# Deferred query/key evictions, column-scalar normalisation steps and later weight casts in a two-layer encoder trunk

## The chip, the cores and the metric

The kernel runs on one core of one Trainium2 chip. The metric is the device time of one execution in microseconds (us). The kernel before was timed three times; the profile is one further execution of the same program. For a kernel of this kind and this spread of runs, about 0.5% (8.4 us) is what a comparison can tell from no change.

## The reference

Two layers over x of 512 rows and 1024 columns, conditioned on one vector c, all in float32:

```
for l in range(2):
    mod = silu(c) @ w_ada[l] + b_ada[l]             # shift1, scale1, gate1, shift2, scale2, gate2
    h = layer_norm(x) * (1 + scale1) + shift1
    proj = h @ w_in[l]                              # q/k/v of 3 head groups | pooling | 2 gates
    outs, lses = dilated_band_attention(...)        # 3 groups, rates 1, 4, 16, centred band, ALiBi
    att = sum(softmax(lses) * outs)                 # groups combined by their denominators
    y_att, y_pool = att @ w_att_out[l], pooled @ w_pool_out[l]
    merged = sigmoid(gate_att) * y_att + sigmoid(gate_pool) * y_pool
    x = layer_norm(ALPHA * x + (1 + gate1) * (merged @ w_o[l]), ln1_g, ln1_b)
    h2 = layer_norm(x) * (1 + scale2) + shift2
    a, b = split(h2 @ w_ffn_in[l])
    x = layer_norm(ALPHA * x + (1 + gate2) * ((silu(a) * b) @ w_ffn_out[l]), ln2_g, ln2_b)
```

## The kernel before

Every weight product is done in three matmuls: each operand is split into a high part (rounded to the matrix engine's float32r form by a cast on ScalarE) and a low part (the rest, by a subtraction on VectorE, `split`, lines 197 to 199), and the matmuls are high by high, high by low and low by high (`mm3`). A weight chunk is 128 by 1024 numbers, loaded by SyncE's queue into one of six `raw` buffers; `weights()` keeps loads seven chunks ahead and splits three chunks ahead. For `w_o` and `w_ffn_out` GpSimd first multiplies the raw chunk by the gate row (line 100).

A *slot* is one projection of 128 output channels over 512 rows: 24 matmuls of 512 columns into one of four PSUM banks called `mm`. `slot()` (line 121) is called ahead of each; it issues what was deferred to it (`self.later`), then one step of every running attention generator (`self.attn`), then a piece of the adaLN product (`self.ada`, line 205). The order in which these Python calls issue instructions is the order in which each engine runs them: nothing reorders it, and an engine that waits holds up all that is behind it.

Stages of a layer, in order: values; pooling; `qk` and attention (four pairs of heads j, six projections q0, k0, q1, k1, q2, k2 each, with the attention of pair j spread over the following eight slots); gates; `merge`; `tail` of the mixing sub-layer; `ffn_in`; `tail` of the feed-forward. An attention step does, among other things, transposes of the probabilities of one block of the step before on TensorE (lines 591 and 601), score matmuls (559 to 565), a masking reduction on VectorE (577) and the exponentials on ScalarE (581). In `qk` a projection's result is evicted from PSUM by ScalarE and VectorE as soon as it has been issued: `query_tiles` (499, 482, 484), `key_tiles` (474, 475, 482, 484, and copies on GpSimd, 491 and 493), `pair_queries` (506, 507), `pair_keys` (GpSimd memsets 517, then 519, 521).

`merge` (line 757) makes eight slots m; after the last gate projection it splits `w_o` chunks 0 to 5 ahead (`prefetch(7, 6)`, line 770), then VectorE multiplies and adds (773, 774), and the merged tile is split. `tail` runs the product with all weights resident, for four row tiles t, by a written script (`TAIL_MIX`, `TAIL_FFN`, `TAIL_END`): `g` is the six matmuls of one weight chunk for one t (794), `c` one step of that t's normalisation `chain` (826), `h` takes the next weight chunk, `n` half a projection of the next stage, which uses the part of h that is ready. The chain's column work is `rstd` (251): a square root on ScalarE (256), then on VectorE four tiny instructions on one number per partition (257, 258, 260, 264), a Newton step of the reciprocal root; then `nm * r` (856), the full-row normalisation on ScalarE (857), transposes (280), scale and shift (867), and the high and low parts of h (868, 872). While the bridge runs, splits of feed-forward chunks have their subtraction on GpSimd (199), not on VectorE.

Of the kernel before, what the change touches and what calls it, by code (L numbers as in the profile page):

```python
# [15 lines left out]
ALU = mybir.AluOpType  # L16
# [13 lines left out]
KD = D // P  # L30
# [18 lines left out]
class Net:  # L49
# [71 lines left out]
    def slot(self):  # L121
        due, keep = [], []
        for e in self.later:
            e[0] -= 1
            (due if e[0] <= 0 else keep).append(e)
        self.later = keep
        for e in due:
            e[1]()
        self.attn = [g for g in self.attn[::-1] if next(g, True) is None][::-1]
        while self.ada:  # L130
            if next(self.ada[0], True) is None:
                break
            self.ada.pop(0)
# [117 lines left out]
    def rstd(self, ss, n=1, scale=1.0 / D):  # L251
        nc = self.nc
        r = self.t("rs", [P, n], F32, 4)
        ve = self.t("ve", [P, n], F32, 4)
        tmp = self.t("nt", [P, n], F32, 4)
        nc.scalar.activation(r, ss, AF.Sqrt, bias=self.eps, scale=scale)
        nc.vector.tensor_scalar(ve, ss, -0.5 * scale, -0.5 * EPS, op0=ALU.mult, op1=ALU.add)
        nc.vector.reciprocal(r, r)
        if n == 1:
            nc.vector.scalar_tensor_tensor(tmp, r, ve, r, op0=ALU.mult, op1=ALU.mult)  # L260
        else:
            nc.vector.tensor_mul(tmp, r, ve)
            nc.vector.tensor_mul(tmp, tmp, r)
        nc.vector.scalar_tensor_tensor(r, tmp, 1.5, r, op0=ALU.add, op1=ALU.mult)  # L264
        return r

    def new_h(self):
# [255 lines left out]

    def qk(self, l, j):
        out = {}
        for nm in ("q0", "k0", "q1", "k1", "q2", "k2"):
            self.slot()
            pb = self.bank()
            self.proj(pb, self.weights(), self.h, range(KD))
            if nm == "k0":  # L530
                out[nm] = self.key_tiles(pb)
            elif nm == "q0":
                out[nm] = self.query_tiles(pb, j)
            elif nm[0] == "q":
                out[nm] = self.pair_queries(pb, self.qsc[:, 4 + j : 5 + j])
            else:
                out[nm] = self.pair_keys(pb)
        return out

    def attention(self, j, x, res):  # L540
# [216 lines left out]
    def merge(self, l, att, ty):  # L757
        nc = self.nc
        out = []
        for m in range(8):  # L760
            self.slot()
            if m % 2 == 0:
                wa = self.weights()
                sg = self.g([P, 2, S])
            pg = self.bank()
            self.proj(pg, self.weights(), self.h, range(KD))
            s = sg[:, m % 2]
            nc.scalar.activation(s, pg, AF.Sigmoid)
            if m == 7:
                self.prefetch(7, 6)  # L770
            py = self.bank()
            self.proj(py, wa, lambda k: att[k], range(4), woff=(m % 2) * S)
            nc.vector.tensor_mul(s, s, py)
            nc.vector.tensor_add(s, s, ty[m])
            mg = self.g([P, 2, S], F32R)
            self.split(mg[:, 0], mg[:, 1], s)
            out.append(mg)
        self.drain()
        return out
# [46 lines left out]
    def chain(self, t, acc, x, g, b, dst, nxt):  # L826
        nc = self.nc
        z, hn = self.g([P, D]), self.g([P, D])
        sm = self.t("sm", [P, 2], F32, 4)
        half = [slice(hf * S, hf * S + S) for hf in range(2)]  # L830
        for hf, c in enumerate(half):
            nc.vector.scalar_tensor_tensor(z[:, c], x[:, c], ALPHA, acc[hf], op0=ALU.mult, op1=ALU.add, accum_out=sm[:, hf : hf + 1])
        nm = self.t("nm", [P, 1], F32, 4)
        ss = self.t("ss", [P, 1], F32, 4)
        nc.vector.tensor_scalar(nm, sm[:, 0:1], sm[:, 1:2], -1.0 / D, op0=ALU.add, op1=ALU.mult)
        nc.scalar.activation(hn, z, AF.Square, bias=nm, scale=1.0, accum_out=ss)
        yield
        nc.vector.scalar_tensor_tensor(x, z, nm, g, op0=ALU.add, op1=ALU.mult)
        yield
        r = self.rstd(ss)  # L840
        yield
        if nxt is None:
            for c in half:
                nc.vector.scalar_tensor_tensor(z[:, c], x[:, c], r, b[:, c], op0=ALU.mult, op1=ALU.add)
                nc.sync.dma_start(out=dst[:, c], in_=z[:, c])
            return
        sm2 = self.t("sm", [P, 2], F32, 4)
        nc.vector.scalar_tensor_tensor(z, x, r, b, op0=ALU.mult, op1=ALU.add, accum_out=sm2[:, 0:1])
        nc.gpsimd.dma_start(out=dst, in_=z)
        nm = self.t("nm", [P, 1], F32, 4)  # L850
        ss = self.t("ss", [P, 1], F32, 4)
        nc.vector.tensor_scalar(nm, sm2[:, 0:1], -1.0 / D, None, op0=ALU.mult)
        nc.scalar.activation(hn, z, AF.Square, bias=nm, scale=1.0, accum_out=ss)
        yield
        r = self.rstd(ss)
        nc.vector.tensor_mul(nm, nm, r)
        nc.scalar.activation(hn, z, AF.Identity, bias=nm, scale=r)
        yield
        pbs = self.h_turn(hn)
        yield  # L860
        tmp = [self.t("q0", [P, 4, P], F32, 2) for _ in range(2)]
        l, which = nxt
        for q in range(2):
            for i in range(4):
                m = 16 * which + 8 * q + 2 * i
                sh, sc = self.mod[:, l, m : m + 1], self.mod[:, l, m + 1 : m + 2]
                nc.vector.tensor_scalar(tmp[q][:, i, :], pbs[q][:, i * P : i * P + P], sc, sh, op0=ALU.mult, op1=ALU.add)
            nc.scalar.copy(self.hA[q][:, :, 0, t * P : t * P + P], tmp[q])
            yield
        for q in range(2):  # L870
            hh = self.hA[q][:, :, :, t * P : t * P + P]
            nc.vector.tensor_sub(hh[:, :, 1], tmp[q], hh[:, :, 0].bitcast(F32))
            yield
# [128 lines left out]
def layout(i):  # L1002
# [20 lines left out]
        "w_ada": c(ada),  # L1023
        "b_col": c(b_col),
        "w_in": c(np.concatenate([v12, v0, qk, rest], axis=1)),
        "w_mix": c(i["w_pool_mix"].transpose(0, 2, 1, 3)),
        "p_col": c(i["pool_scale"].reshape(L, 4, P).transpose(2, 0, 1)),
# [24 lines left out]
```

## Time and profile before

| | us |
|---|---|
| three timed runs | 1685.62, 1688.78, 1692.08 (median 1688.78) |
| the profiled execution | 1687.45 |
| its span (first to last instruction) | 1685.7 |

| engine | busy us | share of the span |
|---|---|---|
| TensorE matmuls (PE) | 1646.1 | 98% |
| TensorE weight loads (PEld) | 1375.5 | 82% |
| VectorE (DVE) | 959.2 | 57% |
| ScalarE (ACT) | 667.3 | 40% |
| GpSimd (POOL) | 336.3 | 20% |

Matmuls overlap: one of 512 columns is shown as 0.39 us, and the next starts about 0.23 us after it. So the busy share of PE counts no time twice, but the time that can go is in the stretches in which the next matmul starts late. The row of PE's waits gives these by what ended them.

### The profile page before, as it was taken

To read this page: it belongs to the slowest core of one execution; us is meant where nothing else is said; L and a number is where in the kernel's file an instruction comes from. 1 tells how busy PE (TensorE), PEld (TensorE's weight loads), DVE (VectorE), ACT (ScalarE), POOL (GpSimd) and SP (SyncE) were. 2 spreads that over 40 slices of the span, in tenths; PEclk is the share of its full clock that TensorE was granted. 3 is DMA by queue.
4 is the path that set the end of the run, shared out by engine and by line. 5 is a ranking of instruction groups with operands and counts; after the bars stand their busy time and mean duration, and the time that the engine had idled before them with its cause. 6 is when DMAs were issued, how large, how long until landed. Compare 5 with 4: busy or idle time off the path is not lost.

```text
span 1685.7 us, 21107 instructions
## 1 busy us (share of the span) xinstructions
PE 1646.1 (98%) x8162; PEld 1375.5 (82%) x8162; DVE 959.2 (57%) x1628; ACT 667.3 (40%) x1118; POOL 336.3 (20%) x325
## 2 busy tenths in 40 slices
PE   8999999999989999999999999999999999999998
PEld 6888887888788888888878888888887888888886
DVE  7568777437775554333573787763477753333335
ACT  6356455623443222221442655555234422222212
POOL 2003222003240000345230122210042300004440
PEclk9999999999999999999999999999999999999999
DMA  9525445233534555332522254443334344233341
GB/s 335 174 75 185 154 138 176 89 100 101 187 100 135 191 189 172 101 112 95 205 90 79 88 188 143 146 156 108 100 113 150 126 154 139 95 100 100 106 144 50
DMA packets 63799, 227.20 MB, mean 135 GB/s; under 512 B 7681, under 2 KB 8097, under 8 KB 63698
## 3 DMA queue, kind: packets, MB, share of 16 engines
q1 hardware_dynamic: 55296, 199.25, 35.4%
q0 software_dynamic: 8400, 26.59, 4.8%
q8 instruction: 64, 1.05, 0.3%
q14 instruction: 37, 0.30, 0.1%
q10 hardware_dynamic: 2, 0.00, 0.0%
HBM read 217.28 MB, written 8.54 MB: 134 GB/s over the span
## 4 chain that ended last, share of the span: by engine, by line
PE 82%; DVE 10%; ACT 5%; issue 2%; DMA 0%; POOL 0%; SPq 0%; DVEq 0%; ACTq 0%
PE mm L239 18%; PE mm L241 18%; PE mm L240 18%; PE mm L794 9%; PE pt L794 5%; PE s L794 4%; PE mm L396 2%; PE mm L625 2%; DVE w L199 2%; PE pt L396 2%; ACT w L198 1%; DVE g L199 1%; DVE nt L260 1%; DVE rs L264 1%; DVE raw L205 1%
## 5 line engine op out<-in xcount | busy, mean ns | idle before, releaser
L239 PE MATMUL mm<-h,w 128*128 128x512 f32 (+1 forms) x1440 | 557.4, 387 | 0.0
L241 PE MATMUL mm<-h,w 128*128 128x512 f32 (+1 forms) x1440 | 554.2, 385 | 1.1 <-DVE w L199 1.1
L240 PE MATMUL mm<-h,w 128*128 128x512 f32 (+1 forms) x1440 | 554.1, 385 | 0.0
L199 DVE TENSOR_TENSOR w<-raw,w 128x1024 fp32r<-128x1024 f32 x238 | 313.8, 1332 | 183.6 <-ACT w L198 183.6
L198 ACT CAST w<-raw 128x1024 fp32r<-128x1024 f32 x250 | 255.5, 1043 | 172.3 <-PE mm L794 145.9
L241 PEld LDWEIGHTS mm<-h,w 128*128 128x128 f32 x1440 | 270.6, 188 | 56.2 <-DVE w L199 1.9
L239 PEld LDWEIGHTS mm<-h,w 128*128 128x128 f32 x1440 | 270.8, 188 | 53.4 <-issue 1.0
L240 PEld LDWEIGHTS mm<-h,w 128*128 128x128 f32 x1440 | 270.8, 188 | 51.8
L100 POOL TENSOR_TENSOR raw<-raw,g 128x1024 f32<-128x1024 f32 x60 | 153.9, 2574 | 376.4 <-DMA raw<-w_ffn_out 222.4
L198 ACT CAST g<-g 128x512 fp32r<-128x512 f32 x76 | 47.1, 620 | 307.2 <-DVE g L890 228.1
L890 DVE TENSOR_TENSOR g<-g,mm 128x512 f32<-128x512 f32 x42 | 28.9, 688 | 211.6 <-PE mm L241 207.4
L794 PE MATMUL mm<-w,g 128*128 128x512 f32 x600 | 143.3, 389 | 0.0
L794 PEld LDWEIGHTS mm<-w,g 128*128 128x128 f32 x600 | 112.6, 188 | 23.3
L205 DVE SCALAR_TENSOR_TENSOR raw<-raw,silc 128x1024 f32<-128x1024 f32 x96 | 118.2, 1237 | 1.4 <-DMA raw<-w_ada 1.4
L199 DVE TENSOR_TENSOR g<-g,g 128x512 fp32r<-128x512 f32 x76 | 66.0, 868 | 62.0 <-ACT g L198 62.0
L794 PE MATMUL s<-w,g 128*128 128x512 f32 x300 | 75.6, 391 | 3.9 <-ACT w L198 2.8
L794 PE MATMUL pt<-w,g 128*128 128x512 f32 x300 | 74.3, 389 | 0.0
L794 PEld LDWEIGHTS s<-w,g 128*128 128x128 f32 x300 | 56.0, 188 | 17.0 <-ACT w L198 3.6
L491 POOL CAST kp<-kp 64x640 fp32r<-64x640 f32 x16 | 21.1, 1342 | 241.0 <-ACT kp L482 241.0
L794 PEld LDWEIGHTS pt<-w,g 128*128 128x128 f32 x300 | 56.3, 188 | 11.7
L232 POOL DMA_DIRECT2D dg<-gr x4 | 2.2, 546 | 295.5 <-DVE gr L230 295.5
L889 ACT ACTIVATE g<-mm 128x512 f32<-128x512 f32 x42 | 25.2, 599 | 85.1 <-PE mm L241 85.1
(233 smaller groups left out, 2061.0 us busy)
## 6 DMA issues: line engine op xcount, KB each, us to landing
raw<-w_in SPq DMA_DIRECT2D x112, 512.0 KB, 3.3
raw<-w_ada SPq DMA_DIRECT2D x96, 512.0 KB, 4.5
raw<-w_ffn_in SPq DMA_DIRECT2D x88, 512.0 KB, 3.4
raw<-w_ffn_out SPq DMA_DIRECT2D x44, 512.0 KB, 3.2
raw<-w_o SPq DMA_DIRECT2D x16, 512.0 KB, 3.3
xs<-g POOLq DMA_DIRECT2D x12, 512.0 KB, 3.0
g<-xs POOLq DMA_DIRECT2D x12, 512.0 KB, 6.4
g<-d POOLq DMA_DIRECT2D x16, 256.0 KB, 4.9
```

Source lines behind the costliest of these rows:

```text
L100: self.nc.gpsimd.tensor_mul(self.raws[i], self.raws[i], self.gate[info(i)][0])
L198: self.nc.scalar.copy(dst_hi, src)
L199: (self.nc.gpsimd if pool else self.nc.vector).tensor_sub(dst_lo, src, dst_hi.bitcast(F32))
L205: self.nc.vector.scalar_tensor_tensor(raw, raw, 1.0, self.silc, op0=ALU.mult, op1=ALU.mult, accum_out=self.mod[:, l, m : m + 1])
L239: mm(out, lhsT=whi, rhs=xhi, start=first, stop=False)
L240: mm(out, lhsT=whi, rhs=xlo, start=False, stop=False)
L241: mm(out, lhsT=wlo, rhs=xhi, start=False, stop=last)
L396: nc.tensor.matmul(pv[p, g], lhsT=hh[:, hi, tk], rhs=w[k][wi][:, c], start=k == 0 and i == 0, stop=k == KD - 1 and i == 2)
L625: nc.tensor.matmul(o, lhsT=v, rhs=rhs, start=b == 0, stop=b == 1)
L794: mm(acc[t][hf], lhsT=src[k][:, part, tk], rhs=wx[:, hf * S : hf * S + S], start=k == 0 and part == 0 and wi == 0, stop=k == K - 1 and par ...
L889: nc.scalar.activation(tmp[:, 0], pa, AF.Silu)
L890: nc.vector.tensor_mul(tmp[:, 1], tmp[:, 0], pb)
```

## The change

Four edits in one:

1. `slot()` steps the attention generators ahead of the deferred work instead of behind it.
2. `qk` defers each eviction by one slot. With edit 1 an eviction stands behind the attention step of the following slot, where it stood ahead of that step. The matmul order does not change.
3. `rstd` for one column, and `nm * r`, use `tensor_scalar` with per-partition scalar operands instead of `scalar_tensor_tensor` and `tensor_mul`. The count of instructions is the same.
4. At the end of `merge`, three `w_o` chunks (2, 3, 4) instead of four are split ahead of the last multiply and add; chunks 5 and 6 are split behind these and ahead of the last merged tile, where chunk 6 came behind the tile.

```diff
@@ slot
         self.later = keep
+        self.attn = [g for g in self.attn[::-1] if next(g, True) is None][::-1]
         for e in due:
             e[1]()
-        self.attn = [g for g in self.attn[::-1] if next(g, True) is None][::-1]
@@ rstd
         if n == 1:
-            nc.vector.scalar_tensor_tensor(tmp, r, ve, r, op0=ALU.mult, op1=ALU.mult)
+            nc.vector.tensor_scalar(tmp, r, ve, r, op0=ALU.mult, op1=ALU.mult)
+            nc.vector.tensor_scalar(r, tmp, 1.5, r, op0=ALU.add, op1=ALU.mult)
         else:
             nc.vector.tensor_mul(tmp, r, ve)
             nc.vector.tensor_mul(tmp, tmp, r)
-        nc.vector.scalar_tensor_tensor(r, tmp, 1.5, r, op0=ALU.add, op1=ALU.mult)
+            nc.vector.scalar_tensor_tensor(r, tmp, 1.5, r, op0=ALU.add, op1=ALU.mult)
@@ qk
-        for nm in ("q0", "k0", "q1", "k1", "q2", "k2"):
-            self.slot()
-            pb = self.bank()
-            self.proj(pb, self.weights(), self.h, range(KD))
+
+        def evict(nm, pb):
             if nm == "k0":
                 out[nm] = self.key_tiles(pb)
...
+        for nm in ("q0", "k0", "q1", "k1", "q2", "k2"):
+            self.slot()
+            pb = self.bank()
+            self.proj(pb, self.weights(), self.h, range(KD))
+            self.defer(1, lambda nm=nm, pb=pb: evict(nm, pb))
         return out
@@ merge
             if m == 7:
-                self.prefetch(7, 6)
+                self.prefetch(7, 5)
             py = self.bank()
             self.proj(py, wa, lambda k: att[k], range(4), woff=(m % 2) * S)
             nc.vector.tensor_mul(s, s, py)
             nc.vector.tensor_add(s, s, ty[m])
+            if m == 7:
+                self.prefetch(7, 7)
             mg = self.g([P, 2, S], F32R)
@@ chain
         r = self.rstd(ss)
-        nc.vector.tensor_mul(nm, nm, r)
+        nc.vector.tensor_scalar(nm, nm, r, None, op0=ALU.mult)
```

The first place is ScalarE in layer 0, in the third slot of pair j=2's projections (q1), where attention j=1 does its third step: `kp_1866` and `kp_1871` are k0's tiles, `pt_1884` the transposed probabilities and `g_1896` the exponentials of block 2. Before:

```order
L198 CAST w_1838<-raw_1563 128x1024
L474 COPY kp_1866<-mm_1835 128x4x64
L482 CAST kp_1871<-kp_1866 64x640
L482 CAST kp_1872<-kp_1866 64x640
L595 COPY g_1883<-pt_1884 128x512
L581 ACTIVATE g_1896,st_1731<-g_1896,st_1731 128x256 x4
L198 CAST w_1928<-raw_1628 128x1024
```

And now, with k0's tiles as `kp_1905` and `kp_1910`, the exponentials as `g_1879`, and q0's eviction (`q_324_1825`, `g_1827`) shown ahead because it stands one step later too:

```order
L500 ACTIVATE q_324_1825<-mm_1756,qsc 128x512
L483 CAST g_1827<-q_324_1825 64x512 x2
L198 CAST w_1838<-raw_1563 128x1024
L600 COPY g_1866<-pt_1867 128x512
L586 ACTIVATE g_1879,st_1721<-g_1879,st_1721 128x256 x4
L475 COPY kp_1905<-mm_1835 128x4x64
L483 CAST kp_1910<-kp_1905 64x640
L483 CAST kp_1911<-kp_1905 64x640
L198 CAST w_1928<-raw_1628 128x1024
```

Three instructions of k0's eviction went from ahead of the exponentials to behind them. VectorE's share of the eviction (copy 475, subtractions 484) moved in the same way behind the masking reductions, and the weight split stays last in the slot.

The second place is VectorE at the end of `merge` in layer 0: `raw_3507`, `raw_3557`, `raw_3566`, `raw_3617`, `raw_3649` and `raw_3700` (now `raw_3705`) are `w_o` chunks 2 to 7, `g_3564` is the sum that becomes the last merged tile, `g_3683` (now `g_3688`) that tile. Before:

```order
L199 TENSOR_TENSOR g_3653<-raw_3507,g_3652 128x1024
L199 TENSOR_TENSOR w_3657<-raw_3557,w_3656 128x1024
L199 TENSOR_TENSOR w_3661<-raw_3566,w_3660 128x1024
L199 TENSOR_TENSOR w_3665<-raw_3617,w_3664 128x1024
L773 TENSOR_TENSOR g_3564<-g_3564,mm_3668 128x512
L774 TENSOR_TENSOR g_3564<-g_3564,g_3135 128x512
L199 TENSOR_TENSOR g_3683<-g_3564,g_3683 128x512
L199 TENSOR_TENSOR w_3709<-raw_3649,w_3708 128x1024
L199 TENSOR_TENSOR g_3715<-raw_3700,g_3714 128x1024
```

And now:

```order
L199 TENSOR_TENSOR g_3652<-raw_3507,g_3651 128x1024
L199 TENSOR_TENSOR w_3656<-raw_3557,w_3655 128x1024
L199 TENSOR_TENSOR w_3660<-raw_3566,w_3659 128x1024
L778 TENSOR_TENSOR g_3564<-g_3564,mm_3663 128x512
L779 TENSOR_TENSOR g_3564<-g_3564,g_3135 128x512
L199 TENSOR_TENSOR w_3681<-raw_3617,w_3680 128x1024
L199 TENSOR_TENSOR w_3685<-raw_3649,w_3684 128x1024
L199 TENSOR_TENSOR g_3688<-g_3564,g_3688 128x512
L199 TENSOR_TENSOR g_3715<-raw_3705,g_3714 128x1024
```

The split of chunk 5 went behind the multiply and add, and that of chunk 6 ahead of the merged tile's. ScalarE's casts stand in the same order, so there too chunk 6's cast is no longer behind the cast that waits for the add.

## Rows read from the trace of the kernel before

**Rows 1.** PE's waits over the span: total us, times, longest us.
```profile
PE s L280 <- ACT g L857: 6.6, 4, 2.8
PE pt L240 <- DVE h L872: 5.5, 2, 2.7
PE pt L601 <- ACT g L581: 5.0, 8, 0.7
...
PE s L794 <- ACT w L198: 2.8, 2, 1.6
...
PE s L794 <- DVE w L199: 1.1, 2, 0.5
```

**Rows 2.** PE's waits in 820 to 870 us, the feed-forward tail of layer 0.
```profile
PE s L280 <- ACT g L857: 2.6, 2, 1.6
PE pt L396 <- DVE h L872: 1.3, 1, 1.3
PE pt L396 <- ACT h L868: 0.7, 1, 0.7
```

**Rows 3.** Busy times by stretch, with the granted clock (PEclk).
```profile
424.00:440.00 16.00, 13.90 (x54) 10.69 (x53) 12.61 (x11) 6.62 (x8) 4.96 (x4) 0.90 0.86 310
440.00:500.00 60.00, 54.48 (x313) 48.30 (x312) 47.96 (x112) 27.59 (x42) 19.46 (x12) 0.97 0.34 113
```

**Rows 4.** Timeline of PE, transposes of block 2: start us, us, instruction, idle before.
```profile
166.56 0.60 PE L601 MATMUL pt<-ident,g 128*128 128x128 f32 x4
...
211.77 0.33 PE L601 MATMUL pt<-ident,g 128*128 128x128 f32 x1 [0.57 <-ACT g L581]
212.76 0.82 PE L601 MATMUL pt<-ident,g 128*128 128x128 f32 x3 [0.66 <-ACT g L581]
```

**Rows 5.** Timeline of ACT just ahead of the second of these.
```profile
207.06 1.48 ACT L482 CAST kp<-kp 64x640 fp32r<-64x640 f32 x2 [2.21 <-DVE kp L475]
...
211.12 0.51 ACT L581 ACTIVATE g<-g,st 128x256 f32<-128x256 f32 x1 [1.98 <-DVE st L577]
```

**Rows 6.** Timeline of PE where merge ends and the tail begins, layer 0.
```profile
428.85 4.24 PE L794 MATMUL s<-w,g 128*128 128x512 f32 x18
434.66 0.73 PE L794 MATMUL s<-w,g 128*128 128x512 f32 x2 [1.57 <-ACT w L198]
435.92 1.32 PE L794 MATMUL s<-w,g 128*128 128x512 f32 x4 [0.53 <-DVE w L199]
```

**Rows 7.** Timeline of DVE at the same place.
```profile
426.71 3.48 DVE L199 TENSOR_TENSOR w<-raw,w 128x1024 fp32r<-128x1024 f32 x3
...
430.83 2.18 DVE L774 TENSOR_TENSOR g<-g,g 128x512 f32<-128x512 f32 x1
```

**Rows 8.** Timeline of POOL at the same place.
```profile
429.13 3.33 POOL L100 TENSOR_TENSOR raw<-raw,g 128x1024 f32<-128x1024 f32 x1 [4.57 <-DVE w L199]
```

**Rows 9.** Timeline of DVE in the mixing tail of layer 0.
```profile
470.62 0.15 DVE L852 TENSOR_SCALAR nm<-sm 128x1 f32<-128x1 f32 x1
470.69 2.71 DVE L872 TENSOR_TENSOR h<-q,h 128x512 fp32r<-128x512 f32 x1
...
474.16 1.51 DVE L260 SCALAR_TENSOR_TENSOR nt<-rs,ve 128x1 f32<-128x1 f32 x1
475.71 2.27 DVE L264 SCALAR_TENSOR_TENSOR rs<-nt,rs 128x1 f32<-128x1 f32 x1
...
478.10 0.68 DVE L872 TENSOR_TENSOR h<-q,h 128x512 fp32r<-128x512 f32 x1
...
482.10 1.75 DVE L260 SCALAR_TENSOR_TENSOR nt<-rs,ve 128x1 f32<-128x1 f32 x1
483.88 2.34 DVE L264 SCALAR_TENSOR_TENSOR rs<-nt,rs 128x1 f32<-128x1 f32 x1
```

**Rows 10.** Timeline of POOL over the first of these.
```profile
469.83 8.15 POOL L199 TENSOR_TENSOR w<-raw,w 128x1024 fp32r<-128x1024 f32 x3 [12.53 <-ACT w L198]
```

**Rows 11.** Groups of DVE by form: count, busy us, mean ns.
```profile
L835 DVE TENSOR_SCALAR nm<-sm 128x1 f32<-128x1 f32 x16 | 3.4, 215 | 0.6
```

## The prediction, made blind

> **What bounds the kernel now.** I read PE's waits first. TensorE sets the end nearly throughout, so time goes only where its next matmul starts late. Of those waits the change can touch five kinds [rows 1]: transposes of attention probabilities that wait for exponentials (L601, eight waits, 5.0 us), the tail's transposes that wait for a normalised row (L280, four, 6.6 us), the bridge's matmuls that wait for a low part of h (L240, two, 5.5 us), and the first tail products that wait for a `w_o` chunk's cast or subtraction (L794, 2.8 and 1.1 us, once each a layer). The feed-forward tail of layer 0 holds 2.6 us of the L280 waits and 2.0 us of its own [rows 2]; so the two mixing tails hold 6.6 - 2.6 = 4.0 of L280 and all 5.5 of L240. Then I read the granted clock: it is 0.90 over the 16 us in which merge ends and 0.97 over the 60 us of the tail behind it, where 1.00 is full speed [rows 3]. At half speed a matmul takes double, so 0.10 x 16 = 1.6 us and 0.03 x 60 = 1.8 us went there; both stretches hold long waits of TensorE, and the fall goes with them.
>
> **Attention (edits 1 and 2).** Four undisturbed transposes of block 2 take 0.60 us. At 211.77 they start 0.57 late and last 212.76 + 0.82 - 211.77 = 1.81, so the pair of waits costs 0.57 + 1.21 = 1.78 us [rows 4]. The eight waits are four such pairs: 7.1 us. ACT shows why: behind k0's two casts, for which it idled 2.21 us and worked 1.48, the exponentials started at 211.12, after a further 1.98 us in which it waited for the reduction on VectorE, itself behind k0's subtractions [rows 5]. TensorE had asked at 211.77 - 0.57 = 211.2. With the eviction behind the step, the 2.21 us of waiting and the 1.48 of casts leave the path of the exponentials. Against that, q0's eviction, which stood ahead of the step before, now falls into the end of that slot: two casts and two subtractions, which I put at the length of k0's casts, 1.48 us. Net 2.21 + 1.48 - 1.48 = 2.2 us earlier, more than the 1.78 that a pair costs. What is late next: the eviction itself and the weight split behind it. The evicted bank is written again only after another projection of 24 matmuls (4.24 / 18 x 24 = 5.7 us [rows 6]) and the next step's scores, and the split is for two slots ahead, so both are covered by about a slot; without that cover each would cost what it comes late. The order in GpSimd's queue changes too: the statistics exchange now stands ahead of k0's copies, whose reader is a later attention. SP's queue is the same. Bounds: 7.1 us gained to 2 us lost (a late split, four times, at the 0.5 us that the one for chunk 6 cost [rows 6]). I take 6.3, nearest to the pair's own price, less 0.2 a pair because the next step's exponentials come closer to TensorE's request.
>
> **End of merge (edit 4).** TensorE waits 1.57 us for chunk 6's cast, 0.53 for its subtraction [rows 6]. Both stand behind the add L774, which took 2.18 us because it ran while GpSimd scaled chunk 7, 429.13 to 432.46 [rows 7, 8]. In the new order chunk 6's cast no longer waits for the add. VectorE has one split fewer ahead of it (3.48 / 3 = 1.16 us each [rows 7]), so it reaches the add earlier, but the add still ends with GpSimd's scaling, which itself waits for a raw buffer; I expect it about 1 us earlier, at 431.5 instead of 433.0. Then come the splits of chunks 5 and 6, 432.7 and 433.8. At 0.23 us a matmul and six a chunk TensorE wants chunk 5's low part at 432.0 and chunk 7's at 435.4, where I get 435.6. So 0.9 us of waiting stays of 2.1 in layer 0, and about 0.5 of 1.7 in layer 1 (2.8 + 1.1 less layer 0's 2.1 [rows 1]). Gain 1.2 + 1.2, and 1.6 of clock in layer 0, since no gap over 1 us is left: 4.0. The two row loads ahead of the tail now stand behind chunk 6's scaling in GpSimd's queue; their first reader is L838, over 10 us later. Bounds: 2.8 + 1.1 + 1.6 = 5.5 gained, to 1 lost if chunk 5, now behind the add, comes as late as chunk 6 did.
>
> **Column forms (edit 3).** Two of the tiny instructions take 1.51 and 2.27 us at 474.16 [rows 9], under three GpSimd subtractions that run from 469.83 to 477.98 [rows 10]: VectorE's operations on two tensors in SBUF get in only between those, at 475.67 and 477.98. L852, a `tensor_scalar` in the same GpSimd stretch, takes 0.15 while the L872 right behind it takes 2.71 [rows 9]. The new forms should take what L835 takes, a `tensor_scalar` with a per-partition operand: 0.215 us [rows 11]. The pair then ends at 474.6, not 477.98, and the L872 that TensorE waits for starts at the next gap, 475.7, instead of 478.10: 2.4 of the 2.7 us of that wait. Twice, 4.8. In the last chain of the tail the pair takes 1.75 + 2.34 [rows 9]; 3.66 us of it goes, but the full-row operation behind is itself on two tensors, so it gains about 2.4, and a third blocked instruction of 1.5 us ahead of L857 goes too. That is about 4 us of chain against an L280 wait of 2.8 in layer 0, where TensorE itself comes 2.4 earlier: I take 2.4 us there and 1.2 in layer 1, its whole wait. With 1.2 of the clock's 1.8 us in layer 0 (the stretch's waits get short), 4.8 + 3.6 + 1.2 = 9.6. Bounds: 5.5 + 4.0 + 1.8 x 2 = 13.1, and 0 if the forms wait as the old ones do.
>
> The Trainium skill's page SBUF — State Buffer (Who interferes with whom) says that VectorE and GpSimd hold a shared port pair as an exclusive lock, which agrees with the rows above; but it lists `tensor_scalar` among the operations that can enter a two-port mode and then contend as well. By that rule the new forms would be held like the old, and this term would be nothing. L852's 0.15 us speaks against it for one column.
>
> In the feed-forward tail of layer 0 the same pair is held again, but its chain goes through further GpSimd stretches, so most of the gain is given back at the next two-tensor operation: of 2.6 + 2.0 us [rows 2] I take 1.5, bounds 0 and 4.6. Layer 1's has no GpSimd work. Where nothing held them, I put the old forms at L852's 0.15 us and the new at L835's 0.215: of 28 + 28 + 12 instructions a dozen were held, and the other 56 grow by 0.065, 3.6 us of VectorE, of which perhaps a seventh is on a path, 0.5.
>
> **Sum.** 6.3 + 4.0 + 9.6 + 1.5 - 0.5 = 20.9. The profiled execution took 1687.45, 1.75 over its span and 1.3 under the median of the runs. 1688.8 - 20.9 = 1668 us for the median.
>
> **Rivals.**
> - *The gain in attention goes to a new wait.* Eviction, copies on GpSimd and the weight split pile up behind the step; the next step's exponentials or a split come late by what the first came early. For it: VectorE's queue runs the reductions, the eviction's subtractions and the weight splits of this stage one behind the other. Against it: a slot of cover. The time: 20.9 - 6.3 = 14.6 gained, 1674.
> - *The column forms are held as well* (the rule above, as a mechanism: any read of SBUF by VectorE waits for GpSimd). Without 9.6 + 1.5 the gain is 9.8 and the time 1679. Against it: L852, and L835 at 0.215 on average with no long one among 16.
> - *Little moves.* The waits named are ended by something else next: the low part by its own two-tensor wait, the chunk by its scaling, the exponentials by the copy of the transposes. Half of each other term gone and attention unmoved leaves under 8 us: 1682. Against it: the three mechanisms are at separate places.
> - *Slower.* The evictions free their PSUM banks late. While an attention holds two of the four `mm` banks, a projection needs the bank of the one before last. If each of the 48 evictions came 0.9 us after TensorE's request, 43 us would be lost: 1688.8 + 43 - 20.9 = 1711. It decides from 20.9 / 48 = 0.44 us of lateness each. Against it: the scores, reductions, exponentials and the eviction itself come to about 6 us behind the projection's end, and the request comes 5.7 us plus the next step's scores behind it, so it is close only where that step is short.
>
> **Chances.** Forecast 0.63 (its own range 1662 to 1673), attention's new wait 0.20, held forms 0.06, little moves 0.08, slower 0.03. All terms at their upper bounds (7.1 + 5.5 + 13.1 + 4.6) would give 1658, which needs all at once; so the range is 1660 to 1679. Faster by over 0.5% (8.4 us, what a measurement here can tell from no change) takes in the first two and most of the third, 0.87; within 0.5% 0.10; slower 0.03.
>
> **What would show it.** Right: no L601 wait left in PE's table; L260 and its successor at about 0.22 us with none over 0.3; L240's waits at 0.5 or less and L280's in the mixing tails under 1; the chunk wait under 1 us and now on a VectorE subtraction; a granted clock near 1.00 from 424 to 440. Wrong: new waits of TensorE on `mm` banks or on L199 in the attention stage; tiny instructions that still last as long as GpSimd's; an add L779 that ends no earlier against the first tail product.

## The result, and the profile after

The changed kernel takes 1663.71 us (median of four runs, 1662.45 to 1665.26). The kernel before took 1689.59 in the same comparison (1685.62 to 1692.08). The ratio is 0.9849, interval [0.9828, 0.9871]: faster by 1.5%, where 1668 us and a range of 1660 to 1679 were forecast. The profiled execution took 1665.26, with a span of 1663.5, against 1687.45 and 1685.7 before.

Both programs run the same 8162 matmuls in the same order, so the difference between the two starts of one matmul says how far the changed kernel is ahead at that place. What this lead gains over a stage, between these two profiled executions:

| stage | forecast, us | lead gained, us |
|---|---|---|
| attention (four steps of block 2) | 6.3 | 1.93 + 1.96 + 1.93 + 1.95 = 7.8 |
| end of merge | 4.0 | 1.9 + 1.3 = 3.2 |
| mixing tails | 9.6 | 7.0 + 5.5 = 12.5 |
| feed-forward tail, layer 0 | 1.5 | -0.9 |
| the rest | -0.5 | -0.3 |
| sum | 20.9 | 22.3 |

The gains in attention and in the mixing tails came out alike in every kernel below that has the same edits and nothing added there. Those at the end of merge and in the feed-forward tail did not: they move with the granted clock of one execution, as shown further on.

PE's waits over the span, total us, times and longest:

```profile
PE s L281 <- ACT g L864: 3.4, 1, 3.4
...
PE s L801 <- DVE w L199: 2.2, 3, 1.0
PE pt L397 <- DVE h L879: 1.1, 1, 1.1
...
PE pt L240 <- DVE h L879: 0.6, 2, 0.3
```

Against [rows 1] the transposes of probabilities (now L606) are gone from the list, the bridge's wait for a low part of h fell from 5.5 to 0.6, and the wait for a chunk's cast became one for a subtraction. The row that was not forecast is the first: one wait of 3.4 us for a normalised row, where there were four.

In attention, TensorE and ScalarE at the place of [rows 4, 5]; PE's row, then ACT's:

```profile
211.35 0.60 PE L606 MATMUL pt<-ident,g 128*128 128x128 f32 x4
```

```profile
208.94 0.51 ACT L586 ACTIVATE g<-g,st 128x256 f32<-128x256 f32 x1 [2.62 <-DVE st L582]
```

The exponentials start at 208.94 instead of 211.12, with TensorE at the same point of the program within 0.3 us: 2.2 us earlier by the two timelines and 2.5 against TensorE's program, where 2.2 was forecast. The four transposes take 0.60 in one piece.

VectorE in the mixing tail of layer 0 at the place of [rows 9], GpSimd over it, and VectorE's groups by form:

```profile
468.63 0.27 DVE L260 TENSOR_SCALAR nt<-rs,ve 128x1 f32<-128x1 f32 x1
468.94 0.21 DVE L261 TENSOR_SCALAR rs<-nt,rs 128x1 f32<-128x1 f32 x1
469.19 0.21 DVE L863 TENSOR_SCALAR nm<-nm,rs 128x1 f32<-128x1 f32 x1
469.32 1.48 DVE L879 TENSOR_TENSOR h<-q,h 128x512 fp32r<-128x512 f32 x1
```

```profile
464.29 8.76 POOL L199 TENSOR_TENSOR w<-raw,w 128x1024 fp32r<-128x1024 f32 x3 [12.43 <-ACT w L198]
```

```profile
L260 DVE TENSOR_SCALAR nt<-rs,ve 128x1 f32<-128x1 f32 x28 | 7.6, 273 | 1.0
L261 DVE TENSOR_SCALAR rs<-nt,rs 128x1 f32<-128x1 f32 x28 | 6.0, 214 | 1.0
```

Under GpSimd's subtractions the three column steps end in 0.8 us, where two of them took 1.51 and 2.27; the two-tensor L879 behind them is still held (1.48, alone 0.68). The longest of the 28 takes 0.275 us in the first group and 0.216 in the second.

The end of merge, to be read against [rows 6 to 8]: VectorE, then GpSimd, then the window of [rows 3].

```profile
420.21 3.07 DVE L199 TENSOR_TENSOR g<-raw,g 128x1024 fp32r<-128x1024 f32 x1 [2.65 <-ACT g L198]
423.20 4.75 DVE L199 TENSOR_TENSOR w<-raw,w 128x1024 fp32r<-128x1024 f32 x2
...
428.58 0.69 DVE L779 TENSOR_TENSOR g<-g,g 128x512 f32<-128x512 f32 x1
```

```profile
416.64 5.56 POOL L100 TENSOR_TENSOR raw<-raw,g 128x1024 f32<-128x1024 f32 x2 [6.31 <-DVE g L199]
...
423.30 2.42 POOL L100 TENSOR_TENSOR raw<-raw,g 128x1024 f32<-128x1024 f32 x1
```

```profile
424.00:440.00 16.00, 14.45 (x62) 11.06 (x61) 14.30 (x21) 4.77 (x8) 2.88 (x4) 1.00 0.82 319
```

The add is no longer held (0.69 instead of 2.18), but GpSimd's scaling now lies over the splits ahead of it: the three subtractions (chunks 2, 3 and 4) take 7.8 us. In the kernel before, the three ahead of the add (chunks 3, 4 and 5, [rows 7]) took 3.5, and the hold fell on the two before these:

```profile
421.51 5.28 DVE L199 TENSOR_TENSOR g<-raw,g 128x1024 fp32r<-128x1024 f32 x2
```

Two waits of TensorE of 1.0 and 0.5 us for them remain in layer 0. The granted clock is 1.00 where it was 0.90; that this is not all the work of edit 4 is shown below.

The feed-forward tail of layer 0, to be read against [rows 2]: PE, VectorE, GpSimd, and two windows of 5 us (the granted clock is the third number from the end).

```profile
834.67 2.81 PE L397 MATMUL pt<-g,h 128*128 128x512 f32 x11 [1.15 <-DVE h L879]
837.31 2.97 PE L397 MATMUL pt<-w,h 128*128 128x512 f32 x12
843.71 1.97 PE L281 MATMUL s<-ident,g 128*128 128x128 f32 x8 [3.43 <-ACT g L864]
```

```profile
832.81 4.60 DVE L879 TENSOR_TENSOR h<-q,h 128x512 fp32r<-128x512 f32 x2 [0.57 <-ACT h L875]
837.34 3.42 DVE L845 SCALAR_TENSOR_TENSOR g<-g,nm,g 128x1024 f32<-128x1024 f32 x1
...
842.17 0.21 DVE L863 TENSOR_SCALAR nm<-nm,rs 128x1 f32<-128x1 f32 x1
```

```profile
829.30 10.37 POOL L199 TENSOR_TENSOR w<-raw,w 128x1024 fp32r<-128x1024 f32 x4 [1.66 <-ACT w L198]
```

```profile
840.00:845.00 5.00, 1.57 (x8) 1.29 (x7) 3.56 (x13) 2.44 (x3) 0.58 (x1) 0.80 0.32 105
845.00:850.00 5.00, 5.00 (x15) 4.01 (x14) 4.61 (x18) 3.43 (x6) 0.00 (x0) 0.52 0.27 107
```

The lead rises here from 12.5 to 16.4, then falls to 11.6. TensorE comes through the first half sooner and then stands before a row that is not ready: row tile 1's column steps (L863) wait on VectorE behind tile 2's L845, which is held by GpSimd's fourth subtraction. With the long gap the granted clock falls to 0.80 and 0.52 in the two windows, 3.4 us of clock in all. In another profiled execution of the same tail (the run with scaling on VectorE, below) the wait is 3.5 us too, but less clock goes:

```profile
840.00:845.00 5.00, 1.65 (x11) 1.54 (x12) 3.35 (x14) 2.77 (x4) 0.58 (x1) 0.97 0.40 132
845.00:850.00 5.00, 5.00 (x17) 3.92 (x17) 4.81 (x18) 3.46 (x6) 0.00 (x0) 0.69 0.21 83
```

That is 1.7 us of clock, and there the lead gains 0.4 over this tail instead of losing 0.9.

### The profile page after: what moved, and what is told of

Read it like the earlier page. It is cut to its first block, busy times and chain, and to the rows that moved or that the text cites. A ratio compares the mean times of both kernels' runs of the same rounds, so it can differ in the third digit from the quotient of the medians.

```text
span 1663.5 us, 21118 instructions
## 1 busy us (share of the span) xinstructions
PE 1639.9 (99%) x8162; PEld 1372.1 (82%) x8162; DVE 948.4 (57%) x1628; ACT 667.2 (40%) x1118; POOL 353.4 (21%) x325
## 4 chain that ended last, share of the span: by engine, by line
PE 89%; DVE 6%; ACT 3%; issue 1%; DMA 0%; POOL 0%; SPq 0%; DVEq 0%; ACTq 0%
PE mm L239 20%; PE mm L241 20%; PE mm L240 20%; PE mm L801 9%; PE pt L801 5%; PE s L801 4%; PE mm L397 2%; PE mm L630 2%; PE pt L397 2%; DVE w L199 1%; PE pt L596 1%; ACT w L198 1%; ACT g L739 1%; PE s L281 1%; PE s L397 1%
## 5 line engine op out<-in xcount | busy, mean ns | idle before, releaser
L240 PE MATMUL mm<-h,w 128*128 128x512 f32 (+1 forms) x1440 | 554.1, 385 | 0.0
L199 DVE TENSOR_TENSOR w<-raw,w 128x1024 fp32r<-128x1024 f32 x238 | 319.5, 1356 | 163.6 <-ACT w L198 163.6
L240 PEld LDWEIGHTS mm<-h,w 128*128 128x128 f32 x1440 | 270.8, 188 | 51.7
L199 DVE TENSOR_TENSOR g<-g,g 128x512 fp32r<-128x512 f32 x76 | 64.5, 848 | 60.7 <-ACT g L198 60.7
```

The source lines that it names most:

```text
L199: (self.nc.gpsimd if pool else self.nc.vector).tensor_sub(dst_lo, src, dst_hi.bitcast(F32))
L240: mm(out, lhsT=whi, rhs=xlo, start=False, stop=False)
```

## The experiments

All times below are medians, except where one run is said; each ratio is to the kernel before in the same comparison.

**Each edit alone.** The kernel before with edits 1 and 2 (the slot and the deferral), with edit 3, and with edit 4, as in the diff above.

> The kernel before with edits 1 and 2 alone (attention step ahead of the deferred eviction). Own place (each edit works in its own stage): all eight L601 waits gone, 4 x 1.95 = 7.8 us less, about 0.5%, nothing moved in merge and in the tails, whose waits stay at L280 6.6 and L240 5.5. Shared gain (the changed kernel's 25.9 us come only when the edits stand together, since each moves what the next one meets): under 4 us, or a wait that appears in merge.

> The kernel before with edit 3 alone (column-scalar forms). Own place: the two mixing tails lose 7.0 + 5.5 = 12.5 us of lateness, the feed-forward tail of layer 0 gives about 1 back, so 11.4 us less, 0.7%; L260 at 0.27 and its successor at 0.21 us everywhere; the L601 and chunk waits stay. Shared gain: under 6 us. Held forms (a column form waits for GpSimd too): no difference, and single L260 above 1 us.

> The kernel before with edit 4 alone. Own place: 1.9 us less in layer 0 and 1.25 in layer 1, 3.2 together (0.2%), the wait for chunk 6's cast gone, a new wait of about 1 us on a VectorE subtraction in layer 0, because the subtractions now run under GpSimd's scaling. Shared gain: no difference or slower by up to 1.3, since the earlier waits on chunk 3's low part are only paid for by what comes behind.

| kernel | us | ratio |
|---|---|---|
| edits 1 and 2 | 1679.3 | 0.9945 [0.9932, 0.9957] |
| edit 3 | 1674.5 | 0.9916 [0.9903, 0.9928] |
| edit 4 | 1684.76 | 0.9979 [0.9968, 0.9991] |

The three gains add up to 0.55 + 0.84 + 0.21 = 1.60%, against 1.51% together: each edit works in its own place, and the shared gain falls. Edit 4's gain is smaller than the 0.5% that was said to be the least to tell; its interval, over nine and fifteen runs, still excludes no change. In the traces, too: edits 1 and 2 alone gain 1.93, 1.96, 1.93 and 1.95 at the same four places, edit 3 alone 7.0 and 5.5 in the two mixing tails.

The profiled execution of edit 4 alone (1689.04, the slowest of its nine) gains 2.3 us at the end of merge in layer 0 and 0.5 in layer 1, where 1.9 and 1.25 were expected. The wait for chunk 6's cast is gone, but waits of 0.9 us (a cast) and 0.5 (a subtraction) stand ahead of the last chunk's product in layer 0, and of 0.8 and 0.5 in layer 1. It is slower than the profiled kernel before all the same: it loses 1.6 us in the feed-forward tail of layer 0, where the tail's transposes wait 4.1 us instead of 2.6, and 1.4 behind layer 1's mixing tail. Neither is a place of edit 4.

Edit 3 alone shows what the clock does by itself. At the end of merge in layer 0 it waits as the kernel before does (1.5 us for a cast, 0.5 for a subtraction, against [rows 6]), and its window of [rows 3] is:

```profile
424.00:440.00 16.00, 13.93 (x60) 10.90 (x59) 13.50 (x13) 7.42 (x9) 5.66 (x4) 1.00 0.88 312
```

The granted clock stays at 1.00 where it was 0.90, and the stage gains 1.65 us without edit 4. So it is in two more kernels below that lack edit 4 and keep such waits (1.3 and 0.5 us, 1.6 and 0.5): the deferral of k0 alone gains 1.86 there, the kernel without GpSimd subtractions 1.58. The same waits came with a fall of the clock in one profiled execution and without one in three.

One reading was not expected. In the profiled execution of edits 1 and 2 (1682.24, the slowest of its six) TensorE waits 2.3 us for a subtraction at the end of merge, which these edits do not touch, and the granted clock falls behind it (0.73 from 425 to 430 us). Its lead goes from 3.4 to -0.7 us; the kernel before has its own waits and its slow clock a little later, so over the stage 0.5 is lost. VectorE, then GpSimd, there:

```profile
420.43 6.55 DVE L199 TENSOR_TENSOR g<-raw,g 128x1024 fp32r<-128x1024 f32 x1 [2.66 <-ACT g L198]
```

```profile
416.67 3.37 POOL L100 TENSOR_TENSOR raw<-raw,g 128x1024 f32<-128x1024 f32 x1 [6.22 <-DVE g L199]
...
421.14 4.76 POOL L100 TENSOR_TENSOR raw<-raw,g 128x1024 f32<-128x1024 f32 x2
```

A subtraction of 1.2 us stood 6.55 us until GpSimd had finished. How the splits meet the scaling is a matter of a microsecond. Whether this, or the clock, is what spreads the runs of one kernel by up to 7 us was not tried.

**The deferral of k0 alone.** Edit 1 stays, and edit 2 is kept for one eviction.

```diff
-            self.defer(1, lambda nm=nm, pb=pb: evict(nm, pb))
+            if nm == "k0":
+                self.defer(1, lambda nm=nm, pb=pb: evict(nm, pb))
+            else:
+                evict(nm, pb)
```

> The kernel before with edits 1 and 2 for k0 alone: the evictions of q0, q1, k1, q2 and k2 stay where they were. If the L601 waits come from k0's casts and subtractions alone, all eight go, as in s_attn (1679), and q0's eviction, which no longer comes in ahead, gives nothing extra. If the deferral of q0 and the others matters too, some of the waits stay: 1683 or more.

Measured: 1679.3 us, 0.9950 [0.9935, 0.9965], the time of edits 1 and 2 in full; the lead gains 1.93, 1.96, 1.93 and 1.95, and no L601 wait is left. The one eviction that stood ahead of block 2's step is the whole gain; deferring the other five neither helps nor harms the time. It does cost head start. With q0's eviction left in its place the exponentials start here:

```profile
207.52 0.51 ACT L588 ACTIVATE g<-g,st 128x256 f32<-128x256 f32 x1 [2.55 <-DVE st L584]
```

Against TensorE's program that is 3.5 us earlier than before, the 2.21 of waiting and the 1.48 of casts nearly in full, where the changed kernel has 2.5.

**Wide column-scalar forms under GpSimd.** In each chain, behind `nm * r`:

```diff
+        nc.vector.tensor_scalar(x[:, 0:S], z[:, 0:S], 2.0, None, op0=ALU.mult)
+        nc.vector.tensor_copy(x[:, S : 2 * S], z[:, S : 2 * S])
```

> The changed kernel with two extra instructions in each row tile's chain, a tensor_scalar and a copy of 128 by 512 numbers from SBUF to SBUF on VectorE, behind nm * r (their result is not used). In the mixing tails the third and fourth tile's stand under a GpSimd subtraction, the first and second tile's do not. If only instructions on two SBUF tensors are held, both last as long in either place, 0.3 to 0.7 us. If wide one-tensor forms contend with GpSimd as well (the rule of the Trainium skill's page SBUF — State Buffer, Who interferes with whom), they last until the end of the subtraction, 1.5 to 2.5 us, under it, and it is the width of one column, not the form, that let the new forms through.

VectorE's rows, first with GpSimd idle, then under its subtractions:

```profile
442.53 0.42 DVE L864 TENSOR_SCALAR g<-g 128x512 f32<-128x512 f32 x1
442.86 0.43 DVE L865 COPY g<-g 128x512 f32<-128x512 f32 x1
...
469.51 1.21 DVE L864 TENSOR_SCALAR g<-g 128x512 f32<-128x512 f32 x1
470.65 2.56 DVE L865 COPY g<-g 128x512 f32<-128x512 f32 x1
```

A `tensor_scalar` and a copy of 512 columns are held like a two-tensor form. The kernel takes 1681.07 us (one run): 24 instructions of 0.4 us cost 17 us, of which 8.1 and 7.4 in the two mixing tails, where they are held. So it was not the form by itself that let the new steps through.

**The same on 2, 8, 32 and 128 columns.**

```diff
+        for w in (2, 8, 32, 128):
+            nc.vector.tensor_scalar(x[:, 0:w], z[:, 0:w], 2.0, None, op0=ALU.mult)
```

> The changed kernel with four extra tensor_scalar behind nm * r in each chain, on 2, 8, 32 and 128 columns, SBUF to SBUF (their result is not used). In s_probe one of 512 columns took 0.42 us alone and 1.2 to 1.5 under GpSimd's subtraction, while nm * r on one column took 0.215 in both. If only a single column escapes, all four last until the subtraction's end or longer than alone; if the hold grows with the work, the narrow ones last as long as alone; if the form with a constant is what is held, and not the width, the one of 2 columns is held too.

```profile
442.37 0.16 DVE L865 TENSOR_SCALAR g<-g 128x2 f32<-128x2 f32 x1
...
469.21 0.21 DVE L863 TENSOR_SCALAR nm<-nm,rs 128x1 f32<-128x1 f32 x1
469.34 0.95 DVE L865 TENSOR_SCALAR g<-g 128x2 f32<-128x2 f32 x1
470.33 2.27 DVE L865 TENSOR_SCALAR g<-g 128x8 f32<-128x8 f32 x1
```

This kernel takes 1679.53 us (one run). Two columns already wait for the end of GpSimd's subtraction (0.95 against 0.16), and one column, right ahead of it and under the same subtraction, does not (0.21). L852 in [rows 9], one column with a constant, was not held either, so it is not the constant. The Trainium skill's page SBUF — State Buffer (Who interferes with whom), by which `tensor_scalar` and copies can take the shared port pair, agrees with the trace from two columns on; for one column the trace shows no hold.

**No GpSimd subtractions.** The kernel before with all weight splits on VectorE:

```diff
-                self.split(hi, lo, raw, info(i) == -1)
+                self.split(hi, lo, raw)
```

> The kernel before with every weight split's subtraction on VectorE, none on GpSimd. If GpSimd's subtractions are what holds the tiny steps, none of L260 and L264 is longer than 0.3 us in the tails, with the old forms; the L240 waits of 5.5 us fall, but VectorE takes 14 to 20 more subtractions of 1.2 us into chains that are on TensorE's path, so the time is between 1680 and 1695. If the tiny steps are long for another reason, they stay at 1.5 to 2.3 us.

VectorE's groups by form, with the old forms:

```profile
L260 DVE SCALAR_TENSOR_TENSOR nt<-rs,ve 128x1 f32<-128x1 f32 x28 | 6.2, 220 | 1.0
L264 DVE SCALAR_TENSOR_TENSOR rs<-nt,rs 128x1 f32<-128x1 f32 x28 | 4.5, 159 | 1.0
```

Before, their means were 583 and 543 ns; now none is longer than 0.23 us. GpSimd's subtractions are the holder. But the kernel takes 1696.12 us, 1.0047 [1.0034, 1.0059], 1 us over the range expected: in VectorE's queue the subtractions wait for casts, and the chains behind them wait too (5.6 us at one place in the feed-forward tail). The hold was worth avoiding with the subtractions left where they are.

**Scaling on VectorE at the end of merge.** Chunks 5 and 6 of `w_o`, in the changed kernel:

```diff
-                self.prefetch(7, 5)
+                self.prefetch(7, 5, 7, self.nc.vector)
...
-                self.nc.gpsimd.tensor_mul(self.raws[i], self.raws[i], self.gate[info(i)][0])
+                (eng or self.nc.gpsimd).tensor_mul(self.raws[i], self.raws[i], self.gate[info(i)][0])
```

> The changed kernel, with the scaling of w_o chunks 5 and 6 at the end of merge on VectorE instead of GpSimd, ahead of the splits of chunks 2 to 4 (a gap of 2.65 us in VectorE's queue stands there). If GpSimd's scaling is what holds VectorE's subtractions there (one of 1.2 us took 3.07, two took 4.75), these take 1.2 each, the chunk waits of 1.6 us in layer 0 and 0.6 in layer 1 go, and the runs scatter less: 1661.5. If the subtractions were late because of their casts or of the load, nothing changes; if VectorE now waits for a load with its whole queue behind it, 2 to 4 us slower.

Measured: 1663.96 us, 0.9861 [0.9845, 0.9877], no difference from the changed kernel, where 1661.5 was expected. VectorE, then GpSimd:

```profile
423.04 4.57 DVE L199 TENSOR_TENSOR w<-raw,w 128x1024 fp32r<-128x1024 f32 x2
```

```profile
422.12 3.26 POOL L100 TENSOR_TENSOR raw<-raw,g 128x1024 f32<-128x1024 f32 x1 [10.44 <-DVE raw L100]
```

Chunk 7's scaling, left on GpSimd, fell on the first of the same two subtractions: it ends at 425.38, and both together took 4.57 us where two take 2.35 alone. The waits went from 1.6 to 1.0 us in layer 0 and stayed at 0.6 in layer 1. The rows agree with GpSimd's scaling as the holder; moving two of the three was not enough, and all three were not tried.

**The order in the feed-forward tail.** Four versions of `TAIL_FFN` in the changed kernel, from `g3 c0x2` on. The first `c1` of each line is row tile 1's second column step and its normalisation.

```diff
- g3 c0x2 g3x2 c0x2 h c2x2 nx2 c1x2 c2x2 nx2 c2 c1 c3 ...     (changed kernel)
+ g3 c0x2 g3x2 c1 c0x2 h c2x2 nx2 c1 c2x2 ...                 (1: ahead of tile 0's low parts)
+ g3 c0x2 g3x2 c0x2 c1 h c2x2 nx2 c1 c2x2 ...                 (2: behind them)
+ g3 c0x2 g3x2 c0x2 h c1 c2x2 nx2 c1 c2x2 ...                 (3: behind the last cast too)
+ g3 c0x2 g3x2 c0x2 h c1 c2x2 nx2 c1x5 c2 nx2 c2 c3x2 nx2 c2 c3 c2x4 c3 nx2 c3 nx2 c3x5 nx6   (4)
```

> The changed kernel, with one step of TAIL_FFN moved: row tile 1's second column step (rstd, nm * r and the normalisation) ahead of the low parts of tile 0 and the full-row operation of tile 2, where it stood behind both. If the 3.4 us wait of the transposes L281 in layer 0's feed-forward tail is only a matter of VectorE's order, the wait goes, the granted clock stays at 1.00 behind it, and about 3.4 + 0.4 + 2.6 = 6 us go: 1657.5. If GpSimd's four subtractions hold the tail whatever the order is, the wait moves to the next row tile and the time stays within 1.5 us of the changed kernel.

> As s_tail, but the moved step stands behind tile 0's two low parts and only ahead of tile 2's full-row operation. In s_tail the step made the first low part miss a gap between two of GpSimd's subtractions: the wait for it went from 1.15 to 3.45 us. If that is so, it is back at about 1.2, the transposes still do not wait, the granted clock stays at 1.00, and 6 us go against the changed kernel: 1657.7. If the tail is bound by the sum of what GpSimd holds, the time stays at that of s_tail, 1662.

> As s_tailA, but the moved step stands behind the last chunk's cast on ScalarE too (in s_tailA that cast waited behind the normalisation, came 6.4 us later, and TensorE waited 1.0 and 1.7 us for that chunk). If the two waits of s_tailA have no other cause, they go and L281 does not wait: 3.4 + 0.4 of waiting and about 2.5 of clock less than the changed kernel, 1657 to 1658. If the tail is bound by what GpSimd holds, another wait takes their place and the time stays above 1661.

> The changed kernel with the later half of TAIL_FFN rewritten. In s_tailC L281 no longer waited for the row (6.1 us ahead of the changed kernel there), but the next row tile's transposes then waited 2.0 us for the scale and shift L874 of the tile before, which freed their PSUM bank, and the granted clock fell behind it: 3.9 of the 6.1 us went back. Here tile 1's scale, shift and parts follow its transposes at once, and tile 2's transposes come after a whole further projection, so neither waits. If the tail is a matter of order alone, the 6 us stay: 1657 to 1658, with a granted clock of 1.00 from 835 to 860. If GpSimd's hold or VectorE's work bounds it, a third wait takes the place and the time stays at 1662 or above.

| version | us (runs) | ratio | lead over this tail on the changed kernel | the same, on the run with scaling on VectorE |
|---|---|---|---|---|
| 1 | 1662.47 (1661.23 to 1663.48) | 0.9842 [0.9829, 0.9855] | -2.3 + 5.9 = 3.6 | 2.3 |
| 2 | 1664.36 (1664.25 to 1664.63) | 0.9864 [0.9845, 0.9882] | 1.6 | 0.3 |
| 3 | 1663.73 (1662.53 to 1664.16) | 0.9854 [0.9840, 0.9869] | 6.5 - 4.3 = 2.2 | 0.8 |
| 4 | 1659.6 (1658.75 to 1659.79) | 0.9835 [0.9818, 0.9853] | 6.5 | 5.2 |

The last column is against an execution of the same tail that lost less clock in it; the medians of versions 2 and 3, which do not differ from the changed kernel's 1663.71, go with that column.

Versions 1 to 3 missed what was expected of them. In each, L281 no longer waited for the row (0.4 us in version 3), and another wait came, each with its own cause. PE's rows of versions 1, 2 and 3:

```profile
837.48 2.79 PE L397 MATMUL pt<-g,h 128*128 128x512 f32 x11 [3.45 <-DVE h L879]
```

```profile
840.70 0.73 PE L397 MATMUL pt<-w,h 128*128 128x512 f32 x2 [1.04 <-ACT w L198]
843.13 0.50 PE L397 MATMUL pt<-w,h 128*128 128x512 f32 x1 [1.70 <-POOL w L199]
```

```profile
848.89 0.79 PE L281 MATMUL s<-ident,g 128*128 128x128 f32 x4 [2.02 <-DVE q L874]
```

In 1 the column steps made the first low part miss a gap between two of GpSimd's subtractions. In 2 the last chunk's cast stood behind the normalisation that waits for those steps. In 3 tile 1's scale and shift, which free the PSUM banks of the next transposes, stood behind tile 2's chain. Version 4 moves them up and puts a whole projection ahead of tile 2's transposes. PE's waits from 820 to 870 us in it, and two windows:

```profile
PE pt L397 <- DVE h L879: 1.2, 1, 1.2
```

```profile
840.00:845.00 5.00, 5.00 (x28) 4.28 (x27) 4.84 (x15) 1.24 (x2) 0.00 (x0) 1.00 0.33 105
845.00:850.00 5.00, 5.00 (x24) 4.14 (x23) 3.04 (x10) 2.37 (x5) 0.58 (x1) 1.00 0.27 108
```

One wait is left, the clock stays at 1.00, and the lead stays. GpSimd's four subtractions run as before (10.4 us), so this stretch was bound by order and not by what they hold. Version 4's five runs all lie under the changed kernel's four, by 2.6 us and more, and the medians differ by 4.1, less than the 6 expected. The two were timed in different comparisons, where the kernel before took 1685.44 and 1689.59, and their ratios overlap, so how much of the 4.1 is the order is not shown by the times; that the wait is gone is shown by the trace. It is the lowest time found.

## Why the prediction was right, and where its terms were off

- *Attention: right, and its price too low.* The pair of waits was priced at 1.78 us and 0.2 of it kept back for the next step's exponentials; the lead shows 1.94 a pair and nothing given back. The 7.8 lie even over the upper bound of 7.1: a matmul is shown as 0.39 us and the next can start 0.23 after it, so an idle time of 0.57 is a start that is 0.73 late, 0.16 more a pair. The 1.48 put down for q0's eviction showed as 1.0 of lost head start, which TensorE did not need. The first rival, a new wait on late evictions or splits (0.20), and the slower one, late PSUM banks, did not show: no L199 or `mm` wait came up in this stage.
- *Column forms: right, with the right mechanism.* Each L240 wait fell by 2.46 us where 2.4 was said, and the 4.0 us of L280 waits went whole where 3.6 was counted. Most of the rest of the 12.5 against 9.6 is the clock. Its cost was taken from one window of layer 0, and 1.2 of it counted. Windows of the kernel before show more, one in layer 0 and two in layer 1:

```profile
495.00:500.00 5.00, 5.00 (x32) 5.00 (x31) 4.32 (x11) 1.24 (x2) 0.00 (x0) 0.67 0.02 7
```

```profile
1310.00:1315.00 5.00, 2.26 (x16) 2.05 (x15) 4.90 (x9) 2.60 (x3) 3.02 (x3) 0.91 0.70 188
1315.00:1320.00 5.00, 5.00 (x34) 5.00 (x33) 4.75 (x5) 1.96 (x4) 5.00 (x2) 0.75 0.52 193
```

  At 0.67, 0.91 and 0.75 these lose 5 x (0.33 + 0.09 + 0.25) = 3.4 us. Both falls come with a wait of 2.7 to 2.8 us, and in the changed kernel's mixing tails, without such waits, the clock is 1.00.
- *The reason given against held forms was right, for one column.* L852's 0.15 us was set against the rule for `tensor_scalar`, and only for one column. The trace agrees with the rule from two columns on, so the edit is safe only because its operands are one column. The rival (0.06) was wrong for this kernel by that margin.
- *End of merge: right in sign, its reason partly wrong.* The add was to end about 1 us earlier against the first tail product. It ends 429.27 - 421.17 = 8.1 us after it, where it was 433.01 - 424.76 = 8.25: what the add no longer waits, the held splits ahead of it took. "An add L779 that ends no earlier" had been named as a sign of being wrong, and it came within 0.15 us of that. The chunk waits fell by 1.6 us (2.1 to 1.6 in layer 0, 1.8 to 0.6 in layer 1) where 2.4 was forecast. The 1.6 of clock came, but as the kernels without edit 4 show, the waits of the kernel before do not always cost it. Of the five profiled executions without edit 4 the clock fell at the end of merge in two, of the nine with it in none; what edit 4 does to the clock is open. In layer 1, where the clock held throughout, those nine gain between 0.3 and 1.3 us.
- *The feed-forward tail: the term that failed.* 1.5 with bounds of 0 and 4.6 was put there, and 0.9 was lost between the two profiled executions. Over the same matmuls (832.98 to 863.28 us in the kernel before) four executions with the old column forms take 30.3, 32.0, 31.9 and 30.3 us, three with the new forms and the same order 31.2, 29.9 and 29.9: from this scatter neither a gain nor a loss is shown. The step that failed is "most of the gain is given back at the next two-tensor operation". Two small waits went, and the lead gained 3.9 us with the slow clock that the kernel before has behind its own. Then the wait for a row, 1.6 us before, was one of 3.4 to 3.5 in all three, so that TensorE's waits in this tail were 4.6 us and are 4.5; and the lower bound left out that a longer gap can also cost clock. Row tile 1's transposes went late because its column steps stood behind a held full-row operation, as versions 3 and 4 show by taking that order away.

The forecast of 20.9 stands against 22.2 between the two profiled executions and 25.9 between the medians. These differ by how each profiled execution stands to its kernel's median: 2.1 under it before, 1.6 over it after. That the sum came so near is in part luck: attention and the mixing tails gave 4.4 us more than forecast, the end of merge and the feed-forward tail 3.2 less.

## What to carry to other kernels

Where two engines can hold each other, go through every instruction in the held stretch by its operands and its width, and ask which of those behind a freed one is still held: a gain ahead of a held instruction comes back as one longer wait. Price a gap of the matrix engine with the clock behind it, from the windows of every such gap and of more than one execution: here the same waits came with 1.6 us of lost clock in one and with none in three. A gain of that size at one place is not an edit's until a kernel without the edit lacks it. Where an order is written by hand, look for the instruction that the waiting one stands behind, and count on two or three further waits behind the first: here three plausible moves failed before one held.

## What the runs showed that was not expected

- A `tensor_scalar` on one column passes under GpSimd's subtraction (0.21 us) and one on two columns does not (0.95 to 1.2 us, alone 0.16). A two-tensor form on one column is held (1.5 to 2.3 us, [rows 9]).
- Between back-to-back subtractions of GpSimd one held instruction got in, so a queue of small ones advanced by one per 1 to 2.9 us: four `tensor_scalar` that take 0.84 us alone took 6.45.
- With two scalar operands read per partition, L260 takes 0.27 us where the old form took 0.22 unheld: dearer, and still worth it.
- The granted clock behind one place of the program differs between executions: at the end of merge waits of 1.3 to 1.6 and 0.5 us came with 0.90 over 16 us in the kernel before and with 1.00 in three other kernels.
